# Scores of the undilated group: the 256-column products as three fp32r products, the edges left in fp32

## The chip, the cores and the metric

The kernel runs on one core of one Trainium2 chip. The metric is the device time of one execution in microseconds; three executions of the kernel before took 908.73, 909.21 and 909.42 us, so the median is 909.21 us. The engines are called PE (TensorE: matrix products and transposes), DVE (VectorE), ACT (ScalarE), POOL (GpSimd) and SP (it issues most of the DMAs).

## The reference, cut to what matters

One encoder layer in float32: 512 tokens, width 1024. After a layer norm, one large projection gives queries, keys and values of two kinds of attention; then come an output projection, a cross-attention to 256 memory tokens and a gated feed-forward layer of width 2816. The change lies in the second kind of attention, the dilated mixture, and there in its first group, the one with dilation 1:

```
DIL_SLOTS = 8
DIL_PAIRS = ((128, 1), (512, 4), (2048, 16))
...
for gi, (window, dil) in enumerate(DIL_PAIRS):
    n_side = window // (2 * dil)
    o, lse = banded_attention(to_residue(qb[:, :, gi], dil)[:, :, :, None],
                              to_residue(kb[:, :, gi], dil),
                              to_residue(vb[:, :, gi], dil), n_side)
```

For group 0 (window 128, dilation 1) a query sees the keys within 64 positions on either side: per head a band of scores `q k^T / 8`, a softmax over the band, and a weighted sum of the values. There are 8 heads of 64 columns in the group, which the kernel takes two at a time, as four chunks of 128 columns (c = 0 to 3). The first kind of attention ("window", 8 query heads on 2 key heads, window 128 on each side, with a sink) is also taken in four chunks.

## The kernel before

**Products.** A float32 product is made in one of two ways. Either both operands are float32 and PE is given one matmul, or both are split into a high part of type fp32r (a rounded copy) and a low part (the rest, fp32r too), and PE is given three fp32r products, high·high, high·low and low·high, which add up in PSUM. The projections are of the second kind: `chunk_fm` (L605) makes one 128 x 512 tile of a projection by 8 x 3 = 24 fp32r matmuls of 512 columns. The weights come by DMA into `raw` tiles, ACT copies them to `hi` (L136), DVE subtracts to get `lo` (L138); there are six buffers of each.

**A projected tile.** `proj` (L614) runs `chunk_fm` and then `rope` (L525), which turns the tile from PSUM into SBUF: DVE multiplies by the cosines (L528) and shuffles (L529), POOL multiplies by the sines (L530) and adds (L531). For the queries and keys of the dilated groups the result of L531 is the float32 tile `Q[key]` that the scores use. For the window attention (`"w"` and `"ka"`) the result is split: POOL copies to the high part (L624), DVE subtracts to get the low part (L625).

**Scores of group 0.** `item_a(c)` (L709) makes the scores of one chunk. The two heads j = 0, 1 lie in the two halves of the partitions (`HJ`), so their matmuls use 64 rows of the PE array each, and each has its own PSUM tile `s[j]`. There are four edge matmuls (two per head) of 64 queries by 128 keys, and three blocks u = 1 to 3 of 128 queries by 256 keys, one float32 matmul for each block and head (L719). Then DVE adds the mask and takes the row minimum (L736), ACT takes exponentials (L739), PE transposes the result (`transposes`, L682, L693), ACT copies the transposes to SBUF (`pT`, L698), and PE multiplies by the values (`pv`, L705). `item_w(c)` (L807) does the same for the window attention, with scores by three fp32r products (L820, the pairs in `PAIRS`). It needs the reciprocal of the softmax sums as a tile over the columns: DVE takes the reciprocals `rd` (L843), ACT spreads them over a 128 x 512 tile `rb` of the x pool (L845), and PE transposes that in four pieces (L859), right behind the twenty transposes of the exponentials (sixteen into two `s` tiles, four into the `t` tile). In the text A0 to A3 are the four items of group 0, W0 to W3 those of the window attention, B0 to B3 those of the two other groups.

**Order.** In the attention part PE runs in exactly the order in which the program was written. That order is made by a queue: the projections are written one behind the other, `mmt` counts each matmul as one tick, and an item at the queue's head goes on when its operands have been `ready` long enough in ticks (`LAG` = 24 behind the projection for the float32 tiles, 30 for the split ones). Each `yield` in an item is such a wait. The orders of ACT, DVE and POOL are not written by hand: when the program is built, a scheduler with its own model of durations sorts the instructions of these engines, and the order that it finds is fixed in the program.

**The x pool.** Tiles of 2 KB per partition for all these parts come from one pool with tag `"x"` and 16 buffers (`XB`, L583). `x_tile` (L585) forces queue items if more than 16 are held; `x_free` gives them back.

## Time and profile before

| | us |
|---|---|
| median of three executions | 909.21 |
| lowest, highest | 908.73, 909.42 |
| profiled execution, its time | 908.85 |
| its span (first to last instruction) | 907.10 |
| PE busy | 894.7 |
| DVE busy | 567.3 |
| ACT busy | 384.8 |
| POOL busy | 130.8 |

The attention part that the change touches lies between about 40 and 345 us of the span. "PE" rows are matmuls and transposes; "PEld" rows are the loads of the stationary operand that go ahead of them. A float32 matmul leaves two records of each kind, an fp32r matmul one. A row of the timeline gives the start, the duration, the engine, the source line, the operation with the tile written and the tiles read, the size, how many equal neighbours were merged into the row (x20), and in square brackets how long the engine sat idle before it and who released it. The end of a matmul is modelled, so the pace is read from start to start.

### The profile page before, as it was taken

Reading aid. Unit: us, or ns where it says so; the run is one execution under the profiler, and the core shown is the slowest. Engines: PE = TensorE matmul, PEld = TensorE weight load, DVE = VectorE, ACT = ScalarE, POOL = GpSimd, SP = SyncE. Lnnn points to the kernel's source line nnn. Section 1 sums busy time; section 2 is a strip of 40 time slices with the busy share of each in tenths; the row PEclk is TensorE's granted clock in tenths of the full one; section 3 lists DMA queues with packets and bytes.
Section 4 is the critical chain, followed back from the end, with each engine's and each line's share of the span. In section 5 each row is a group of like instructions: output and inputs, shape, how many; then the busy total and the mean of one; then the engine's idle time right before and its main releaser. Section 6 shows DMA issues by size and latency. Waiting matters only on the chain.

```text
span 907.1 us, 13008 instructions
## 1 busy us (share of the span) xinstructions
PE 894.7 (99%) x5147; PEld 769.8 (85%) x5147; DVE 567.3 (63%) x968; ACT 384.8 (42%) x672; POOL 130.8 (14%) x111
## 2 busy tenths in 40 slices
PE   8999999999999999999999999999999999999996
PEld 7778988898888898788988889899999999888885
DVE  7976146435456667879466576987777767433347
ACT  4563436415545576315454224454444445222200
POOL 1064134332454420010000010000000000000001
PEclk9999999999999999999999999999999999999999
DMA  6762041214221337416222304333333354233201
GB/s 222 228 209 70 25 139 48 73 67 117 70 70 47 94 117 232 140 47 176 80 70 70 94 25 123 88 94 93 101 109 94 98 158 139 94 94 102 82 24 69
DMA packets 117086, 92.84 MB, mean 102 GB/s; under 512 B 12488, under 2 KB 101024, under 8 KB 117026
## 3 DMA queue, kind: packets, MB, share of 16 engines
q1 hardware_dynamic: 116192, 89.80, 32.8%
q10 hardware_dynamic: 834, 2.22, 0.6%
q8 instruction: 40, 0.66, 0.3%
q14 instruction: 20, 0.16, 0.1%
HBM read 87.82 MB, written 4.19 MB: 101 GB/s over the span
## 4 chain that ended last, share of the span: by engine, by line
PE 92%; DVE 4%; DMA 1%; ACT 1%; issue 1%; POOL 0%; DVEq 0%; ACTq 0%
PE g L168 52%; PE s L168 25%; PE o L168 5%; PE t L168 4%; PE o L705 3%; PE s L693 2%; PE s L208 1%; DVE lo L138 1%; DMA vt<-in_ln_in_g_dram 0%; DMA raw<-in_w_up_dram 0%; ACT hi L136 0%; DVE lo L282 0%; DVE oA L348 0%; PE s L1241 0%; DVE st L312 0%
## 5 line engine op out<-in xcount | busy, mean ns | idle before, releaser
L138 DVE TENSOR_TENSOR lo<-raw,hi 128x1024 fp32r<-128x1024 f32 x126 | 159.8, 1270 | 91.1 <-ACT hi L136 90.4
L136 ACT CAST hi<-raw 128x1024 fp32r<-128x1024 f32 x126 | 132.3, 1051 | 145.0 <-PE g L168 86.6
L168 PE MATMUL g<-Thi,hi 128*128 128x512 f32 x240 | 94.8, 395 | 0.0
L168 PE MATMUL g<-Tlo,hi 128*128 128x512 f32 x240 | 94.2, 393 | 0.0
L168 PE MATMUL g<-Thi,lo 128*128 128x512 f32 x240 | 94.0, 392 | 0.0
L109 POOL TENSOR_TENSOR rs<-ve,mhalf 128x1 f32<-128x1 f32 x18 | 15.3, 851 | 521.6 <-DVE ve L115 513.4
L530 POOL TENSOR_TENSOR zs<-zs,rsn 128x512 f32<-128x512 f32 x29 | 56.9, 1963 | 144.6 <-DVE zs L529 131.2
L168 PE MATMUL g<-Uhi,hi 128*128 128x512 f32 (+1 forms) x216 | 74.3, 344 | 0.0
L168 PE MATMUL g<-Ulo,hi 128*128 128x512 f32 (+1 forms) x216 | 74.0, 342 | 0.0
L168 PE MATMUL g<-Uhi,lo 128*128 128x512 f32 (+1 forms) x216 | 73.9, 342 | 0.0
L168 PE MATMUL g<-hi,Thi 128*128 128x512 f32 x184 | 71.6, 399 | 0.0
L168 PE MATMUL g<-hi,Tlo 128*128 128x512 f32 x184 | 71.0, 395 | 0.5 <-DVE Tlo L1189 0.5
L168 PE MATMUL g<-lo,Thi 128*128 128x512 f32 x184 | 70.6, 395 | 0.4 <-DVE lo L282 0.4
L528 DVE TENSOR_TENSOR zs<-g,rc 128x512 f32<-128x512 f32 x29 | 19.9, 687 | 62.1 <-PE g L168 39.6
L168 PE MATMUL g<-x,hi 128*128 128x256 f32 x320 | 58.8, 284 | 0.0
L168 PEld LDWEIGHTS g<-Thi,hi 128*128 128x128 f32 x240 | 45.1, 188 | 10.4 <-issue 0.8
L168 PEld LDWEIGHTS g<-Tlo,hi 128*128 128x128 f32 x240 | 45.1, 188 | 9.7 <-issue 0.8
L168 PEld LDWEIGHTS g<-Thi,lo 128*128 128x128 f32 x240 | 45.1, 188 | 9.3
L168 PEld LDWEIGHTS g<-x,hi 128*128 128x128 f32 x320 | 50.0, 192 | 0.5 <-issue 0.3
L168 PE MATMUL s<-Ulo,hi 128*128 128x512 f32 (+1 forms) x136 | 49.5, 364 | 0.0
L168 PE MATMUL s<-Uhi,hi 128*128 128x512 f32 (+1 forms) x136 | 49.5, 364 | 0.0
L168 PE MATMUL s<-Uhi,lo 128*128 128x512 f32 (+1 forms) x136 | 49.5, 364 | 0.0
(378 smaller groups left out, 2075.7 us busy)
## 6 DMA issues: line engine op xcount, KB each, us to landing
raw<-in_w_in_dram SPq DMA_DIRECT2D x37, 512.0 KB, 3.8
raw<-in_w_gate_dram SPq DMA_DIRECT2D x22, 512.0 KB, 3.8
raw<-in_w_up_dram SPq DMA_DIRECT2D x22, 512.0 KB, 4.0
raw<-in_w_down_dram SPq DMA_DIRECT2D x22, 512.0 KB, 3.5
raw<-in_w_xk_dram SPq DMA_DIRECT2D x8, 512.0 KB, 3.8
raw<-in_w_xv_dram SPq DMA_DIRECT2D x8, 512.0 KB, 3.4
raw<-in_w_xq_dram SPq DMA_DIRECT2D x8, 512.0 KB, 4.6
raw<-in_w_xo_dram SPq DMA_DIRECT2D x8, 512.0 KB, 3.5
```

Of the source, the lines that this page charges most:

```text
L109: nc.gpsimd.tensor_tensor(out_, in_, mhalf, ALU.pow)
L136: nc.scalar.copy(hi, raw)
L138: (eng or nc.vector).tensor_tensor(lo, raw, hi.bitcast(F32), ALU.subtract)
L168: on_pe(nc.tensor.matmul(o, l, r, start=first, stop=last))
L208: on_pe(nc.tensor.transpose(ps[:, i // 4, f : f + P], t[:, i * P : (i + 1) * P], ident))
L528: nc.vector.tensor_tensor(zc, ps, rc, ALU.mult)
L530: nc.gpsimd.tensor_tensor(sh, sh, rsn, ALU.mult)
L693: nc.tensor.transpose(tp[:, k, :], s_, ident)
L705: nc.tensor.matmul(o[HJ[j], t0:t1], lhs(j), rhs(j), start=i == 0, stop=i == len(parts) - 1)
```

## The change

The keys and queries of group 0 (`key[1] == 0`) are now split in `proj` like those of the window attention: POOL makes the high part (8 casts of 128 x 512 more), DVE the low part (8 subtractions of 128 x 512 more), and they count as ready 30 ticks after the projection instead of 24. The float32 tile is kept as the third part. In `item_a` each of the six 256-column float32 matmuls of a chunk becomes three fp32r products; the loop over the two heads moves inside, so that a block is done for both heads before the next. The four edge matmuls of a chunk still use the float32 tiles. A chunk's key and query so hold three tiles of the x pool each instead of one, and the pool grows from 16 to 18 buffers, wherever it is used.

```diff
-            raw = [xpool.tile([P, 1, 512], F32, tag="x", bufs=16, name="raw") for _ in range(2)]
+            raw = [xpool.tile([P, 1, 512], F32, tag="x", bufs=18, name="raw") for _ in range(2)]
...
-    XB = 16
+    XB = 18
...
         ps = chunk_fm(key, wt)
-        if key[0] not in ("w", "ka"):
+        group = key[0] not in ("w", "ka")
+        if group and key[1]:
             Q[key] = x_tile([P, S], F32, key)
             rope(ps, view, Q[key])
             ready[key] = now[0] + LAG
             return
-        raw = x_tile([P, S], F32, "raw")
+        raw = x_tile([P, S], F32, key if group else "raw")
         rope(ps, view, raw)
         hi, lo = Q[key] = dest or [x_tile([P, S], F32R, key) for _ in range(2)]
         nc.gpsimd.tensor_copy(hi, raw)
         nc.vector.tensor_tensor(lo, raw, hi.bitcast(F32), ALU.subtract)
-        x_free("raw")
+        if group:
+            Q[key] = (hi, lo, raw)
+        else:
+            x_free("raw")
         ready[key] = now[0] + LAG + 6
...
-                mm(s[j][o0 : o0 + 64, 0, 0:P], q[HJ[j], q0 : q0 + 64], k[HJ[j], kk0 : kk0 + P], True, True)
+                mm(s[j][o0 : o0 + 64, 0, 0:P], q[2][HJ[j], q0 : q0 + 64], k[2][HJ[j], kk0 : kk0 + P], True, True)
         for u in range(1, 4):
             bk, c0 = cols[u]
-            for j in range(2):
-                mm(
-                    s[j][:, bk, c0 : c0 + 256],
-                    q[HJ[j], 128 * u - 64 : 128 * u + 64],
-                    k[HJ[j], 128 * (u - 1) : 128 * (u + 1)],
-                    True,
-                    True,
-                )
+            for i, (m, n) in enumerate(PAIRS):
+                for j in range(2):
+                    mm(
+                        s[j][:, bk, c0 : c0 + 256],
+                        q[m][HJ[j], 128 * u - 64 : 128 * u + 64],
+                        k[n][HJ[j], 128 * (u - 1) : 128 * (u + 1)],
+                        i == 0,
+                        i == 2,
+                    )
```

The same 16 becomes 18 in two later uses of the pool, in the feed-forward layer. In PE's order the scores of A0, A2 and A3 now stand six projection matmuls later than before, A1 where it stood. The twenty-four transposes of each W item stand in PE's order as before, those of W1 six matmuls later; the four of the tile `rb` are still the last of them. The orders of the other engines changed with the build. Line numbers of the changed kernel are up to 5 higher than those of the kernel before (L693 is now L697, L698 is L702, L845 is L850, L862 is L867, L624 and L625 are L625 and L626).

On ACT, around the transposes of W0, these rows stood before. `x<-rd` is the copy that makes `rb`, `pT` are the copies of the transposed exponentials, `fw` is the copy of the transposed `rb`:

```order
L136 CAST hi<-raw 128x1024
L845 COPY x<-rd 128x512
L698 COPY pT<-s 128x512 x4
L698 COPY pT<-t 128x512
L862 COPY fw<-o 128x512
L669 COPY vg<-g 128x512
```

Now the same place reads:

```order
L136 CAST hi<-raw 128x1024
L702 COPY pT<-s 128x512 x4
L702 COPY pT<-t 128x512
L850 COPY x<-rd 128x512
L867 COPY fw<-o 128x512
L673 COPY vg<-g 128x512
```

The copy that makes `rb` moved from ahead of the five `pT` copies to behind them.

On ACT, around the transposes of W1, this stood before (the first row is the last three exponentials of W1):

```order
L833 ACTIVATE pu,dnW<-pu,ast 128x385 x3
L136 CAST hi<-raw 128x1024
L845 COPY x<-rd 128x512
L698 COPY pT<-s 128x512 x4
L698 COPY pT<-t 128x512
L862 COPY fw<-o 128x512
```

And this stands there now:

```order
L838 ACTIVATE pu,dnW<-pu,ast 128x385
L136 CAST hi<-raw 128x1024
L838 ACTIVATE pu,dnW<-pu,ast 128x385 x2
L136 CAST hi<-raw 128x1024
L702 COPY pT<-s 128x512 x2
L850 COPY x<-rd 128x512
L702 COPY pT<-s 128x512 x2
L702 COPY pT<-t 128x512
L867 COPY fw<-o 128x512
```

Here the copy that makes `rb` moved behind the first two `pT` copies, and two casts of weights moved up, one of them in between the exponentials. In W2 and W3 it stands ahead of the `pT` copies, as before.

On POOL, at the start of the attention part, the rope and the split of the first tiles stood like this before (`x_466` is the key of chunk 0, `x_496` its query, `kah_435` the high part of the window attention's key):

```order
L530 TENSOR_TENSOR zs_98<-zs_98,rsn_71 128x512
L531 TENSOR_TENSOR x_466<-zs_98 128x512
L530 TENSOR_TENSOR zs_98<-zs_98,rsn_71 128x512
L531 TENSOR_TENSOR x_496<-zs_98 128x512
L530 TENSOR_TENSOR zs_98<-zs_98,rsn_71 128x512
L531 TENSOR_TENSOR x_564<-zs_98 128x512
L624 CAST kah_435<-x_564 128x512
```

And like this now (`x_500` is the query, `x_471` and `x_505` are the two high parts):

```order
L530 TENSOR_TENSOR zs_98<-zs_98,rsn_71 128x512
L531 TENSOR_TENSOR x_466<-zs_98 128x512
L625 CAST x_471<-x_466 128x512
L530 TENSOR_TENSOR zs_98<-zs_98,rsn_71 128x512
L531 TENSOR_TENSOR x_500<-zs_98 128x512
L625 CAST x_505<-x_500 128x512
L530 TENSOR_TENSOR zs_98<-zs_98,rsn_71 128x512
L531 TENSOR_TENSOR x_540<-zs_98 128x512
L625 CAST kah_435<-x_540 128x512
```

Each tile's cast stands right behind the addition that makes it, so the rope of the query comes one cast later. On DVE the two low parts of chunk 0 (L626) stand behind the weights' subtraction that follows the query's shuffle, and behind the shuffle of the next tile; the second of them is ahead of the next weights' subtraction (L138).

## The prediction

> **What bounds the kernel now.** I read the page first, then the waits of PE in the attention part, then the timelines of PE, ACT, POOL and DVE around the items that the change touches. On the page PE is busy nearly all the time, and the chain that ended last is PE work:

> ```profile
> PE 894.7 (99%) x5147; PEld 769.8 (85%) x5147; DVE 567.3 (63%) x968; ACT 384.8 (42%) x672; POOL 130.8 (14%) x111
> PE 92%; DVE 4%; DMA 1%; ACT 1%; issue 1%; POOL 0%; DVEq 0%; ACTq 0%
> ```

> All waits of PE between 40 and 345 us are three:

> ```profile
> PE s L168 <- POOL x L531: 0.5, 1, 0.5
> PE s L693 <- ACT pu L785: 0.3, 1, 0.3
> PE s L168 <- DVE x L625: 0.2, 1, 0.2
> ```

> So in this part a microsecond of PE work that goes is a microsecond won, and a microsecond for which PE waits is one lost; the other engines count only where PE waits for them. Half a microsecond of waiting is already in A0, where the scores wait for the query.

> **The scores.** In A0 the timelines of PE and of PEld show one chunk (eight records of the four edge matmuls, twelve of the six large ones):

> ```profile
> 55.62 0.39 PE L168 MATMUL g<-Tlo,hi 128*128 128x512 f32 x1
> 55.85 0.39 PE L168 MATMUL g<-Thi,lo 128*128 128x512 f32 x1
> 56.70 1.95 PE L168 MATMUL s<-x 64*64 64x128 f32 x20 [0.46 <-POOL x L531]
> 58.57 0.50 PE L168 MATMUL g<-Thi,hi 128*128 128x512 f32 x1
> ```

> ```profile
> 56.69 0.21 PEld L168 LDWEIGHTS s<-x 64*64 64x64 f32 x8 [0.88 <-POOL x L531]
> 57.07 1.17 PEld L168 LDWEIGHTS s<-x 64*128 64x128 f32 x12 [0.17 <-issue]
> ```

> The large ones last from 57.07 to the next projection matmul at 58.57, which is 1.50 us. What three fp32r products cost at this shape stands in W1, whose first two blocks have 64 rows and 256 columns too, two heads at a time (a row x4 holds two products):

> ```profile
> 149.23 0.39 PE L168 MATMUL s<-kah,x 64*128 64x256 f32 x2
> 149.45 0.28 PE L168 MATMUL s<-kal,x 64*128 64x256 f32 x2
> 149.57 0.40 PE L168 MATMUL s<-kah,x 64*128 64x256 f32 x4
> 149.81 0.28 PE L168 MATMUL s<-kal,x 64*128 64x256 f32 x2
> ...
> 150.75 0.33 PE L168 MATMUL t<-kal,x 64*128 64x384 f32 x1
> 150.92 0.34 PE L168 MATMUL t<-kah,x 64*128 64x384 f32 x1
> 151.19 0.50 PE L168 MATMUL g<-Tlo,hi 128*128 128x512 f32 x1
> ```

> The first pair takes 0.22 us (149.45 - 149.23), each further one 0.12 (149.57 - 149.45, and 0.24 for two up to 149.81). The last one before a projection costs 0.10 more than its pace (151.19 - 150.92 = 0.27 against 150.92 - 150.75 = 0.17). Nine pairs: 0.22 + 8 x 0.12 + 0.10 = 1.28 us. Saved: 1.50 - 1.28 = 0.22 us a chunk, **0.88 us** in four. Bounds: 0.32 a chunk if the edges ahead hide the 0.10 by which the first pair is slower, 0.02 if that is paid at each of the three blocks. I take 0.22, since a W item pays it once.

> **A0's wait.** How soon scores can follow a projection is seen in A2, where they waited for nothing:

> ```profile
> 136.53 0.39 PE L168 MATMUL g<-Thi,lo 128*128 128x512 f32 x1
> 136.85 1.95 PE L168 MATMUL s<-x 64*64 64x128 f32 x20
> ```

> That is 0.32 us, so in A0 they could have begun at 55.85 + 0.32 = 56.17 and lost 56.70 - 56.17 = 0.53. The new order puts six projection matmuls ahead, 6 x 0.23 = 1.38 (pace from 55.62 to 55.85), so they can begin at 57.55. POOL and DVE at this place:

> ```profile
> 49.18 1.30 POOL L530 TENSOR_TENSOR zs<-zs,rsn 128x512 f32<-128x512 f32 x1 [21.14 <-DVE zs L529]
> 50.56 2.35 POOL L531 TENSOR_TENSOR x<-zs 128x512 f32<-128x512 f32 x1
> 53.11 2.17 POOL L530 TENSOR_TENSOR zs<-zs,rsn 128x512 f32<-128x512 f32 x1 [0.20 <-DVE zs L529]
> 55.36 1.28 POOL L531 TENSOR_TENSOR x<-zs 128x512 f32<-128x512 f32 x1
> ...
> 61.39 0.61 POOL L624 CAST kah<-x 128x512 fp32r<-128x512 f32 x1
> ```

> ```profile
> 52.92 1.21 DVE L138 TENSOR_TENSOR lo<-raw,hi 128x1024 fp32r<-128x1024 f32 x1
> ...
> 56.95 0.72 DVE L529 STREAM_SHUFFLE zs<-g 128x512 f32<-128x512 f32 x1
> ...
> 63.71 0.67 DVE L625 TENSOR_TENSOR kal<-x,kah 128x512 fp32r<-128x512 f32 x1
> ```

> The key's tile ends at 52.91, its cast (0.61), 0.08 behind as POOL's operations follow each other in these rows, at 53.60, so the query's rope begins at 53.68 instead of 53.11 and its tile ends at 57.21 instead of 56.64. That is ahead of 57.55: the edges don't wait. They take 57.07 - 56.69 = 0.38, to 57.93. The query's cast ends at 57.21 + 0.08 + 0.61 = 57.90, DVE is done with the shuffle at 57.67, and its subtraction ends about 57.95 + 0.67 = 58.62. The block's third product needs it, and would begin at 57.93 + 0.22 + 0.12 = 58.27; with the 0.05 that PE took after POOL's end (56.69 - 56.64) it begins at 58.67. Lost: 0.40 instead of 0.53, a gain of **0.13**. Bounds: no wait at all, a gain of 0.53; or one more DVE subtraction of 1.21 in the way, a loss of 1.08.

> The POOL rows show how uncertain that is: the same operation took 1.30 us alone and 2.17 beside the DVE subtraction. [...]

> In the other chunks the split is early enough. The other 6 casts and 6 subtractions (0.61 and 0.67 us each) lie in gaps of POOL and DVE, a projection or more ahead of their use. The pool of 18 buffers costs nothing that I can see: PE never waits for one now.

> **The moved copies.** This is the largest term. ACT and DVE around W0:

> ```profile
> 89.06 0.61 ACT L845 COPY x<-rd 128x512 f32<-128x512 f32 x1
> 91.86 2.05 ACT L698 COPY pT<-s 128x512 f32<-128x512 f32 x4 [2.19 <-PE s L693]
> 93.78 0.63 ACT L698 COPY pT<-t 128x512 f32<-128x512 f32 x1
> 94.25 0.64 ACT L862 COPY fw<-o 128x512 f32<-128x512 f32 x1
> ```

> ```profile
> 88.25 0.20 DVE L843 RECIPROCAL rd<-dnW 128x8 f32<-128x8 f32 x1 [1.25 <-ACT pu L833]
> ```

> and PE's transposes of `rb`, load and product:

> ```profile
> 92.87 0.47 PEld L859 LDWEIGHTS o<-cst,x 128*128 128x128 f32 x4
> ```

> ```profile
> 92.97 0.60 PE L859 MATMUL o<-cst,x 128*128 128x128 f32 x4
> ```

> Before, `rb` was made at 89.06, three microseconds ahead of need. Now its copy stands behind five `pT` copies, and the first of these waits for PE's transposes. It then takes the slot that `fw` had: it starts at 94.25 and ends at 94.86, and PE's load can begin at 94.91 instead of 92.87. PE executes in order, so the projection behind it waits too: **2.04 us** lost. The values' products of W0 come 14 projection matmuls later and stay covered.

> In W1 two `pT` copies stand ahead of it:

> ```profile
> 160.11 2.06 ACT L698 COPY pT<-s 128x512 f32<-128x512 f32 x4 [2.58 <-PE s L693]
> 162.02 0.63 ACT L698 COPY pT<-t 128x512 f32<-128x512 f32 x1
> ```

> ```profile
> 161.22 0.60 PE L859 MATMUL o<-cst,x 128*128 128x128 f32 x4
> ```

> A copy there takes (162.02 - 160.11) / 4 = 0.48. `rb` would start at 160.11 + 0.96 = 161.07, end at 161.68 and let the load begin at 161.73; it needs 161.22 less the 0.10 between load and product in W0. Lost: **0.61 us**. Bounds of the two together: 2.4 (PE could use an overlap of 0.1 each) to 3.0 (the weight cast put ahead of W1's copies delays them).

> **The sum.** -0.88 - 0.13 + 2.04 + 0.61 = +1.64 us. Against the profiled execution's 908.85 that is 910.5; its time lies 0.36 below the median of the three, so against the median it is 909.21 + 1.64 = 910.9 us, 0.18% more. A measurement of this kernel can tell about 0.2%, here 1.8 us, from no change. Moved to its bounds alone, the scores' term gives 910.5 to 911.7, A0's 910.5 at the low end, the copies' 910.6 to 911.2; all low ends together give 909.8.

> **The rivals.** *The copy is not in the way.* `rd` is there at 88.45, and ACT then idles 2.19 us. If ACT took the ready copy ahead of the waiting ones, no stall would come: -0.88 - 0.13 gives 908.2 us. Against it: before, too, ACT stood idle in front of its first `pT` copy, and no row shows it passing over a waiting instruction; it could not, though, be seen there, as nothing behind was ready. [...] Chance 0.07.

> *POOL and DVE get in each other's way in A0.* If one more 1.21 us subtraction lies ahead of the query's low part, A0 costs 1.08 instead of gaining 0.13: 909.21 + 1.64 + 1.21 = 912.1 us, slower beyond doubt. It decides from 0.2 us on, since 1.64 is so near 1.8. For it: the spread from 1.30 to 2.17. Against it: the new order puts the low part ahead of the next weights' subtraction. Chance 0.16.

> *The products are not cheaper.* If nine pairs behind float32 edges cost as much as six float32 ones, 0.88 is gone: 911.7 us. W1 speaks against it. Chance 0.03.

> **The numbers.** The forecast has 0.74. In it the time passes 1.8 us more in somewhat over a third of the cases (0.27), by the bounds; with the second rival and most of the third, slower has 0.45. Faster needs the first rival and a far better A0: 0.02. The rest, 0.53, is within 0.2%. The range leaves out the first rival and goes 0.2 us, the least distance of an execution from the median of the three, beyond the low ends together (909.8) and the second rival (912.1): 909.6 to 912.3.

> **What would show it.** In the changed profile: PE idle about 2 us ahead of the transposes of `rb` in W0 and 0.6 in W1, released by the ACT copy; A0's scores waiting for the low part, some 0.4 us; the large products of a chunk 1.28 us from first load to the next projection. No wait of PE for ACT in W0 would make the forecast wrong, and so would one of more than half a microsecond anywhere else.

## The result, and the profile after

The changed kernel takes **915.48 us** (median of six, 912.76 to 916.17) against 908.8 us for the kernel before (908.4 to 909.42): a ratio of 1.0066 on record, with a 95% interval from 1.0056 to 1.0075 (that of the two medians is 1.0074). It is slower by 6.7 us where 1.7 were forecast, and beyond the range. The profiled execution took 915.7 us with a span of 913.6; that of before took 908.85 with a span of 907.1. So 6.85 us have to be found, 6.5 in the span and 0.35 outside it.

The page of the changed kernel shows PE busy for 4.3 us more than before, though its work was to shrink, and idle for 2.2 us more (the span's 6.5 less those 4.3):

```profile
PE 899.0 (98%) x5171; PEld 773.2 (85%) x5171; DVE 576.7 (63%) x976; ACT 384.7 (42%) x672; POOL 136.1 (15%) x119
PE 90%; DVE 4%; ACT 2%; DMA 1%; issue 1%; POOL 1%; DVEq 0%; ACTq 0%; POOLq 0%
```

The waits of PE (total, times, longest) give the idle part. Two rows are new at the top, and they are the two places of the forecast. They make 3.8 us; the 0.5 us of A0's wait before and a wait of 1.1 us for a DMA at the start of the program are gone, which leaves 2.2:

```profile
PE o L864 <- ACT x L850: 2.3, 2, 1.8
PE s L168 <- DVE x L626: 1.5, 2, 1.3
```

The first is the transposes of `rb` in W0 and W1, the second the scores' wait for a low part, nearly all of it in A0.

The busy part is the surprise. Cut into the stretches of 3.41 us at whose edges the granted clock changes, the windows of the changed kernel show it in the column PEclk, the third from the end (PE's busy time is the first value after the stretch's length):

```profile
58.18:61.60 3.42, 1.98 (x27) 1.43 (x20) 3.06 (x2) 0.64 (x1) 3.28 (x4) 1.00 0.96 386
61.60:65.01 3.41, 3.41 (x9) 2.63 (x9) 3.41 (x18) 2.25 (x10) 1.38 (x1) 0.50 0.41 122
65.01:68.42 3.41, 3.41 (x22) 2.96 (x22) 3.38 (x8) 2.86 (x10) 0.81 (x2) 1.00 0.20 61
95.73:99.14 3.41, 1.58 (x11) 1.34 (x10) 0.69 (x1) 2.61 (x6) 1.15 (x2) 1.00 0.36 107
99.14:102.56 3.42, 3.42 (x10) 2.73 (x9) 0.00 (x0) 0.73 (x2) 0.00 (x0) 0.50 0.00 0
102.56:105.97 3.41, 3.41 (x30) 2.13 (x31) 0.00 (x0) 0.00 (x0) 0.00 (x0) 1.00 0.00 0
```

In 58.18 to 61.60 PE is idle for 1.44 us, in 95.73 to 99.14 for 1.83 us, and behind each of them stands one stretch at half the clock, in which 9 or 10 matmuls are done. By offsets (the start of the same 128x512 product in the two traces) 1.71 us are lost in the first and 1.52 in the second, and the page counts them as busy. In the kernel before, the clock reads full from 3.97 us to 905 us.

Not every execution has both. Two of the six took 912.76 us at a mean granted clock of 0.997, the other four 915.25 to 916.17 us at 0.993 to 0.995. Two such windows alone take 2 x 3.41 x 0.5 / 913.6 = 0.0037 off that mean, so in the two shorter ones at least one window was missing; only the 915.7 was profiled.

A0 on PE, with the wait for the low part and the projection's slow matmuls behind it:

```profile
58.56 0.50 PE L168 MATMUL s<-x 64*128 64x256 f32 x4 [0.17 <-POOL x L625]
60.34 1.09 PE L168 MATMUL s<-x 64*128 64x256 f32 x14 [1.27 <-DVE x L626]
61.36 0.62 PE L168 MATMUL g<-Thi,hi 128*128 128x512 f32 x1
61.78 0.63 PE L168 MATMUL g<-Tlo,hi 128*128 128x512 f32 x1
```

Those come every 0.42 us here and came every 0.23 before. What the scores waited for is on DVE, and beside it, on POOL, the next rope's first step:

```profile
58.54 1.74 DVE L626 TENSOR_TENSOR x<-x 128x512 fp32r<-128x512 f32 x1 [0.49 <-POOL x L625]
60.20 2.31 DVE L138 TENSOR_TENSOR lo<-raw,hi 128x1024 fp32r<-128x1024 f32 x1
```

```profile
57.90 0.61 POOL L625 CAST x<-x 128x512 fp32r<-128x512 f32 x1
58.47 1.27 POOL L530 TENSOR_TENSOR zs<-zs,rsn 128x512 f32<-128x512 f32 x1
```

POOL goes from the query's cast straight to the rope of `ka` at 58.47. DVE's subtraction starts at 58.54 and takes 1.74 us, where the same operation took 0.67 in the profile of before.

W0 on ACT and on PE. The copy of `rb` (L850) stands behind five `pT` copies:

```profile
94.85 2.06 ACT L702 COPY pT<-s 128x512 f32<-128x512 f32 x4 [2.69 <-PE s L697]
96.76 0.63 ACT L702 COPY pT<-t 128x512 f32<-128x512 f32 x1
97.24 0.66 ACT L850 COPY x<-rd 128x512 f32<-128x512 f32 x1
```

```profile
97.95 0.66 PE L864 MATMUL o<-cst,x 128*128 128x128 f32 x4 [1.83 <-ACT x L850]
98.37 0.60 PE L168 MATMUL g<-lo,Thi 128*128 128x512 f32 x1
...
169.34 0.66 PE L864 MATMUL o<-cst,x 128*128 128x128 f32 x4 [0.44 <-ACT x L850]
```

The projection behind W0's transposes waited with them, until 98.37. The last row is W1, with 0.44 us. The scores themselves came out as forecast; in A2, from the first large load to the next projection's product:

```profile
144.98 1.13 PEld L168 LDWEIGHTS s<-x 64*128 64x128 f32 x18 [0.17 <-issue]
```

```profile
146.25 0.50 PE L168 MATMUL g<-Thi,hi 128*128 128x512 f32 x1
```

146.25 - 144.98 = 1.27 us, where the forecast had 1.28.

### The profile page after: what moved, and what is told of

Same layout as the page of the kernel before. It is cut to its first block, busy times and chain, and to the rows that moved or that the text cites. A ratio compares the mean times of both kernels' runs of the same rounds, so it can differ in the third digit from the quotient of the medians.

```text
span 913.6 us, 13069 instructions
## 1 busy us (share of the span) xinstructions
PE 899.0 (98%) x5171; PEld 773.2 (85%) x5171; DVE 576.7 (63%) x976; ACT 384.7 (42%) x672; POOL 136.1 (15%) x119
## 4 chain that ended last, share of the span: by engine, by line
PE 90%; DVE 4%; ACT 2%; DMA 1%; issue 1%; POOL 1%; DVEq 0%; ACTq 0%; POOLq 0%
PE g L168 50%; PE s L168 24%; PE o L168 5%; PE t L168 4%; PE o L709 3%; PE s L697 2%; DVE lo L138 1%; ACT hi L136 1%; PE s L208 1%; DMA vt<-in_ln_in_g_dram 0%; DMA raw<-in_w_up_dram 0%; POOL x L531 0%; DMA raw<-in_w_in_dram 0%; ACT pT L702 0%; DVE lo L282 0%
## 5 line engine op out<-in xcount | busy, mean ns | idle before, releaser
L138 DVE TENSOR_TENSOR lo<-raw,hi 128x1024 fp32r<-128x1024 f32 x126 | 161.7, 1286 | 94.3 <-ACT hi L136 93.6
L168 PE MATMUL g<-Thi,hi 128*128 128x512 f32 x240 | 95.4, 398 | 0.0
L168 PE MATMUL g<-Tlo,hi 128*128 128x512 f32 x240 | 95.0, 396 | 0.0
L168 PE MATMUL g<-Thi,lo 128*128 128x512 f32 x240 | 94.5, 394 | 0.0
L530 POOL TENSOR_TENSOR zs<-zs,rsn 128x512 f32<-128x512 f32 x29 | 53.8, 1856 | 141.9 <-DVE zs L529 135.9
L168 PE MATMUL g<-Uhi,hi 128*128 128x512 f32 (+1 forms) x216 | 74.3, 344 | 0.0
L168 PE MATMUL g<-Ulo,hi 128*128 128x512 f32 (+1 forms) x216 | 74.0, 342 | 0.0
L168 PE MATMUL g<-Uhi,lo 128*128 128x512 f32 (+1 forms) x216 | 73.9, 342 | 0.0
L168 PE MATMUL g<-hi,Thi 128*128 128x512 f32 x184 | 72.2, 402 | 0.0
L168 PE MATMUL g<-hi,Tlo 128*128 128x512 f32 x184 | 71.6, 399 | 0.5 <-DVE Tlo L1194 0.5
L168 PE MATMUL g<-lo,Thi 128*128 128x512 f32 x184 | 71.4, 399 | 0.4 <-DVE lo L282 0.4
L168 PE MATMUL g<-x,hi 128*128 128x256 f32 x320 | 58.8, 284 | 0.0
L168 PEld LDWEIGHTS g<-Thi,hi 128*128 128x128 f32 x240 | 45.5, 190 | 10.2 <-issue 0.5
L168 PEld LDWEIGHTS g<-Thi,lo 128*128 128x128 f32 x240 | 45.5, 190 | 9.5
L168 PEld LDWEIGHTS g<-Tlo,hi 128*128 128x128 f32 x240 | 45.4, 189 | 9.5 <-issue 0.5
L168 PEld LDWEIGHTS g<-x,hi 128*128 128x128 f32 x320 | 50.0, 192 | 0.5 <-issue 0.3
L168 PE MATMUL s<-Uhi,hi 128*128 128x512 f32 (+1 forms) x136 | 49.5, 364 | 0.0
L168 PE MATMUL s<-Ulo,hi 128*128 128x512 f32 (+1 forms) x136 | 49.5, 364 | 0.0
L168 PE MATMUL s<-Uhi,lo 128*128 128x512 f32 (+1 forms) x136 | 49.5, 364 | 0.0
```

The lines of the kernel that those rows point to most:

```text
L138: (eng or nc.vector).tensor_tensor(lo, raw, hi.bitcast(F32), ALU.subtract)
L168: on_pe(nc.tensor.matmul(o, l, r, start=first, stop=last))
L530: nc.gpsimd.tensor_tensor(sh, sh, rsn, ALU.mult)
```

## The experiments

Two theories stood against each other. **Theory H**: a long wait of TensorE costs its length, and then a window of 3.41 us at half the clock. **Theory L**: a wait costs its length and nothing else, and what is missing is in the new work. A second question was why A0's low part came late. Where the text counts offsets, it is by the start of the same 128x512 product in two traces.

### The copy of rb put back ahead

```diff
-        nc.scalar.copy(
+        rbc = nc.scalar.copy(
             rb.rearrange("p b (j d) -> p (b j) d", j=2),
...
-        t0, *t1, t3, t2 = transposes(
+        with tc.issue_after(rbc.ins):
+            t0, *t1, t3, t2 = transposes(
```

> The changed kernel with one thing put back: in the sink group's items the copy of the reciprocals (rb) stands ahead of the five pT copies on ScalarE again, as it did before the change. Theory H (a long wait of TensorE costs its own length and then a 3.41 us window at half the granted clock, 1.7 us more): W0's wait of 1.83 us and W1's of 0.44 us go, the half-clock window behind W0 goes, the one behind A0 stays; 915.5 - 1.83 - 0.44 - 1.7 = 911.5 us. Theory L (a wait costs its length and nothing else, and the missing 3.4 us are in the new work itself, so they stay): 915.5 - 2.3 = 913.2 us.

Measured: **909.79 us** (909.24 to 912.08), 1.0016 of before (1.0007 to 1.0025). ACT of this kernel has the copy ahead of the transposes' copies again, and PE's list of waits has no row for L850:

```profile
90.07 0.62 ACT L850 COPY x<-rd 128x512 f32<-128x512 f32 x1
92.85 2.06 ACT L702 COPY pT<-s 128x512 f32<-128x512 f32 x4 [2.16 <-PE s L697]
```

The gain is 5.7 us, more than the 4.0 of theory H and far more than the 2.3 of theory L, which falls: the waits that went are 2.3 us long. The rest is not one half-clock window but two. A0's wait is as long as it was, but in the profiled execution the grid of windows falls so that 1.27 us of idle time lie in one of them, and the next keeps the full clock:

```profile
57.35:60.77 3.42, 2.15 (x28) 1.36 (x27) 3.10 (x3) 1.24 (x1) 3.28 (x4) 1.00 0.96 340
60.77:64.18 3.41, 3.41 (x20) 2.74 (x17) 3.41 (x16) 1.84 (x9) 1.73 (x2) 1.00 0.41 137
```

Six of the eleven times lie between 909.24 and 909.79, the other five between 910.66 and 912.08, about a half-clock window higher, as if A0's wait costs its window in some executions and not in others. The mean granted clock fits it, 0.997 to 0.999 in the six and 0.995 to 0.997 in the five, but only one of them was profiled, so that reading is argued.

### A0's scores 14 products later

```diff
-        ready[key] = now[0] + LAG + 6
+        ready[key] = now[0] + LAG + 6 + (14 if group and key[2] == 0 else 0)
```

> The changed kernel with A0's scores asked for 14 chunk matmuls (some 3.2 us) later, so that the query's low part is there in time; all else as it is. Theory H: A0's wait of 1.44 us goes, and the half-clock window behind it with its 1.7 us; the one behind W0 stays: 915.5 - 1.44 - 1.7 = 912.4 us. Theory L: 915.5 - 1.4 = 914.1 us.

Measured: **913.5 us** (913.1 to 914.05), 1.0051 (1.0039 to 1.0063), between the two. The wait for the low part is gone, but the edit put another in its place, so its time decides nothing. A0's softmax (L741 on DVE) came so late that the normalisation of the memory rows went ahead of it, and PE's transposes waited for it:

```profile
PE s L697 <- DVE stT L741: 2.4, 1, 2.4
```

```profile
62.65 1.29 DVE L131 BATCH_NORM_STATS2 st<-oB 128x6 f32<-128x512 f32 x2 [0.51 <-DMA oB<-in_mem_dram]
...
66.87 0.28 DVE L741 CUSTOM_DVE_ANT_0 pu<-s,cst 128x128 f32<-128x128 f32 x1
```

What it does show is the grid. The new wait is cut in two by it (1.46 and 1.08 us idle), W0's 1.83 us too (its larger part leaves 1.50), and no window at half clock follows either:

```profile
64.86:68.27 3.41, 1.95 (x9) 1.29 (x7) 3.41 (x13) 2.46 (x7) 0.57 (x1) 1.00 0.09 28
68.27:71.69 3.42, 2.34 (x15) 1.74 (x16) 2.97 (x10) 3.42 (x14) 1.52 (x3) 1.00 0.00 0
71.69:75.10 3.41, 3.41 (x23) 2.60 (x23) 1.13 (x3) 2.08 (x4) 0.19 (x1) 1.00 0.55 159
95.58:98.99 3.41, 1.91 (x10) 1.91 (x11) 0.46 (x1) 2.04 (x4) 0.00 (x0) 1.00 0.00 0
98.99:102.41 3.42, 3.42 (x22) 2.71 (x22) 0.00 (x0) 0.59 (x1) 0.00 (x0) 1.00 0.00 0
```

### Both edits

> The changed kernel with both edits: rb's copy ahead of the pT copies, and A0's scores 14 chunk matmuls later. Theory H: no window at half clock inside the program, and only the cheaper scores are left: 908.8 - 0.88 - 0.46 (A0's wait of the kernel before goes too) = 907.5 us, up to 908.4 if A0 keeps half a microsecond of wait. Theory L: 915.5 - 2.3 - 1.4 = 911.8 us.

Measured: **912.08 us** (911.37 to 912.25), 1.0033 (1.0021 to 1.0045). That is near theory L's number, but not for its reason: the softmax's wait is here too, this time in one window, and the next runs at half clock.

```profile
67.26:70.67 3.41, 0.97 (x8) 0.86 (x9) 3.41 (x19) 3.01 (x13) 0.43 (x1) 1.00 0.00 0
70.67:74.09 3.42, 3.42 (x12) 2.59 (x13) 1.03 (x1) 2.62 (x8) 1.33 (x3) 0.50 0.33 95
```

The edit that was meant to free A0 was a bad one; the experiment with `va` below frees it in another way.

### The kernel before, with W0's copy made late

```diff
+        if c == 0:
+            with tc.issue_after(pcopy[0].ins):
+                spread()
         two = ps_tile("o", 1, [P, 4, P])
```

(`spread` holds the copy of `rb`, `pcopy[0]` the last `pT` copy; the other items call it where it stood.)

> The kernel before the change with one thing spoiled: in W0 alone the copy of the reciprocals stands behind the five pT copies on ScalarE. None of the change's products, splits or buffers is in it. Theory H: TensorE waits some 1.8 us in W0 and the next 3.41 us window runs at half the granted clock: 908.8 + 1.8 + 1.7 = 912.3 us. Theory L: 908.8 + 1.8 = 910.6 us and no such window. Rival: the half clock needs the change's longer scores as well as a wait; then also 910.6 us.

Measured: **911.02 us** (910.28 to 912.73), 1.0026 (1.0017 to 1.0035). The profiled execution, the 912.73, shows the wait and the window:

```profile
PE o L869 <- ACT x L849: 1.8, 1, 1.8
```

```profile
93.25:96.67 3.42, 1.59 (x12) 1.35 (x11) 0.00 (x0) 2.62 (x6) 0.63 (x1) 1.00 0.36 104
96.67:100.08 3.41, 3.41 (x10) 2.66 (x10) 0.00 (x0) 0.83 (x2) 0.00 (x0) 0.50 0.00 0
```

Just ahead of W0 it stands 0.60 us behind the kernel before, after the window 4.18: of these 3.58 us, 2.06 come at the wait and 1.52 in the window. So neither the change's products nor its splits are needed for the half clock; the rival falls. The median of the times, 2.4 us over before, is less than that, and the lowest is 1.6 us over. In four of the other executions (910.86 to 911.43 us) the mean granted clock is 0.999, and one such window alone would bring it to 1 - 3.41 x 0.5 / 911 = 0.998: there the wait cost no window. For the rest that stays open, as they weren't profiled.

### No rope beside the query's low part

`va` is projected ahead of `ka`, with the copy of `rb` put back ahead as above.

```diff
-        proj(("ka",), w_cols(w_in, KA), NAT, kaT)
         proj_va()
+        proj(("ka",), w_cols(w_in, KA), NAT, kaT)
```

> The changed kernel with the rb copy ahead of the pT copies, and with va projected ahead of ka, so that no rope addition of GpSimd stands beside the subtraction that makes the query's low part (va needs none). Theory P (the subtraction took 1.74 us because GpSimd's next rope step ran beside it): the subtraction takes 0.69 us again, A0's second wait falls from 1.27 to 0.2 or 0.3 us, and no window runs at half clock in any run; 909.5 - 1.0 = 908.5 us. Rival: the subtraction is slow for another reason, such as its place behind DVE's own work; the wait stays and the time too, 909.8 us.

Measured: **908.47 us** (907.19 to 909.54), 1.0001 (0.9992 to 1.001). The subtraction of the query's low part and PE's wait for it:

```profile
58.39 0.69 DVE L626 TENSOR_TENSOR x<-x 128x512 fp32r<-128x512 f32 x1 [1.86 <-POOL x L625]
```

```profile
59.14 1.10 PE L168 MATMUL s<-x 64*128 64x256 f32 x14 [0.22 <-DVE x L626]
```

0.69 us and 0.22 us, as theory P had them; the rival falls. In the profiled execution no window at half clock is left inside the program (mean granted clock 0.997, half only behind the end of PE's work). The key's low part, which still has a rope step beside it, still takes 1.77 us, but PE doesn't wait for that one. This is the changed kernel with both of its side effects mended, and it isn't measurably faster than the kernel before.

### Chunk 0 left in fp32

Chunks 1 to 3 have the three products, chunk 0 the code of before; the copy of `rb` stands ahead.

```diff
-        if group and key[1]:
+        if group and (key[1] or key[2] == 0):
```

> The changed kernel with the rb copy ahead of the pT copies, and chunk 0 left as it was before (fp32 scores, no split), so that only chunks 1 to 3 have the three products. A0's wait should be that of the kernel before, 0.5 us. By the sum: three times 0.22 us saved, and some 0.35 us more that the changed kernels spend outside the span: 908.66 - 0.66 + 0.35 = 908.35 us. Rival: the saving is an illusion of where I cut the rows, and the time is 909.0 us.

Measured: **908.46 us** (907.99 to 909.17), 0.9997 (0.9988 to 1.0005). That is 0.1 us from the sum and 0.5 from the rival. The interval reaches to 909.1 us, so the time alone doesn't exclude the rival; the offsets do, by which its A1, A2 and A3 save 0.18, 0.25 and 0.23 us.

### The buffers alone

```diff
-    XB = 16
+    XB = 18
```

(and the four other uses of 16)

> The kernel before the change with 18 of the x buffers in place of 16, and nothing else. Theory: the buffers cost nothing in the span and nothing outside it, 908.66 us, and what the changed kernels spend more outside the span (2.13 against 1.78 us) comes with their instructions. Rival: the buffers bring the 0.35 us, 909.0 us; or they let transfers start sooner and change the span by a few tenths either way.

Measured: **908.78 us** (907.59 to 909.51), 1.0003 (0.9994 to 1.0012), with 1.76 to 1.85 us outside the span. The buffers cost nothing that can be measured.

### Waits put into a dense stretch

```diff
             gemm_fm(pg, wg, h2T, 0, S)
+            if f in HOLD:
+                for i in range(HOLD[f]):
+                    nc.scalar.copy(dz[:, 0:512], pg)
+                nc.tensor.transpose(ps_tile("t", 1)[:, 0:P], dz[:, 0:P], ident)
             gemm_fm(pu, wu, h2T, 0, S)
```

with `HOLD = {6: 1, 8: 2, 10: 3, 12: 2, 14: 3, 16: 4, 18: 2, 20: 3, 21: 6}`.

> The kernel before the change with nine waits put into TensorE's stream in the gate and up products, where its matmuls otherwise stand end to end: after a gate product one to six ScalarE copies in a row of the finished tile, and a TensorE transpose that needs the last of them, so that TensorE stands still for some 0.9 us (one copy) to 4 us (six). The output stays what it was. Theory H: where the idle time inside one 3.41 us window of the clock's grid is over some 1.5 us the next window runs at half the granted clock, where it is less none does, and a wait of 2 us may go free when the grid cuts it in two. Rival: the half clock belongs to the attention items with their short fp32 matmuls; here no window but those with over 3 us of idle time is followed by one.

Measured: 930.44 us in the profiled execution, 928.63 in the other. Three of the nine waits, window by window:

```profile
638.44:641.85 3.41, 1.40 (x7) 0.90 (x6) 1.92 (x2) 2.97 (x5) 0.00 (x0) 1.00 0.28 84
641.85:645.26 3.41, 3.41 (x9) 2.64 (x9) 1.50 (x2) 0.93 (x2) 0.00 (x0) 0.50 0.53 154
710.12:713.53 3.41, 1.67 (x8) 1.05 (x6) 1.89 (x3) 2.53 (x4) 0.00 (x0) 1.00 0.48 139
713.53:716.95 3.42, 2.53 (x12) 2.12 (x13) 1.87 (x3) 1.73 (x4) 0.00 (x0) 1.00 0.51 151
734.01:737.42 3.41, 1.75 (x8) 1.13 (x6) 1.89 (x3) 2.45 (x4) 0.00 (x0) 1.00 0.49 145
737.42:740.84 3.42, 1.84 (x9) 1.53 (x10) 1.20 (x2) 2.15 (x4) 0.00 (x0) 1.00 0.48 143
```

The window with 2.01 us of idle time (3.41 - 1.40) halves the next, and the rival, for which it took 3 us or the attention items, falls. Windows with 1.74 and 1.66 us don't, nor does a wait of 3.2 us that the grid cuts into 1.66 and 1.58. So theory H is right in kind, but its 1.5 us isn't a fixed limit: 1.44 us sufficed behind A0 in the changed kernel, 1.74 didn't here. What else than idle time decides it stays open.

The ends of the programs narrow it down, where PE's work stops within a window of the grid. The kernel before kept the full clock behind a window with 1.81 us of idle time; the one with W0's copy made late lost it behind 1.89:

```profile
898.26:901.67 3.41, 1.60 (x14) 1.40 (x12) 2.04 (x6) 0.00 (x0) 0.26 (x1) 1.00 0.00 0
901.67:905.09 3.42, 0.00 (x0) 0.00 (x0) 2.50 (x6) 0.00 (x0) 0.66 (x1) 1.00 0.25 90
902.21:905.63 3.42, 1.53 (x13) 1.33 (x12) 2.05 (x6) 0.00 (x0) 0.34 (x1) 1.00 0.00 0
905.63:909.04 3.41, 0.00 (x0) 0.00 (x0) 2.42 (x6) 0.00 (x0) 0.58 (x1) 0.50 0.27 97
```

Other ends agree: 1.75 us (the changed kernel) and 1.77 (the doubled products below) kept it, 2.39 (18 buffers) and 2.40 (`va` ahead) lost it; the mean granted clock of these two executions, 0.997 each for 0.999 in the kernel before, fits that. In the whole traces of before and after, and in the windows given here of the others, every window with 1.83 us or more idle was followed by one at half clock, and none with 1.81 or less was, but for the 1.44 behind A0. The work in that one is A0's score products of 64 rows. Whether these count for less was not tested; the same products with 1.27 us idle, in the kernel with the copy put back, kept the clock.

### What lies outside the span

In every profiled or timed execution of the kernel before, 1.74 to 1.86 us lie between its time and its span; in the changed kernel and its variants with all four chunks split, 2.0 to 2.2. Four kernels looked for it. The first two are the kernel before with eight one-column fills on POOL, and with each of the 24 large score products issued twice (the second writes the same values).

```diff
+            if not key[1]:
+                nc.gpsimd.memset(small, 0.0)
```

> The kernel before the change with eight more GpSimd instructions and nothing else: a one-column fill behind the rope of each key and query of the undilated group, eight in all, as many as the change adds in casts. The question is the time outside the span, 1.78 us in every run of the kernel before and 2.13 us in those of the changed kernel. If it comes with GpSimd's instructions it is 2.1 us here; if not, 1.78 us. The span should stay at 906.8 us, within the few tenths by which single runs differ.

```diff
-            for j in range(2):
+            for j in (0, 1, 0, 1):
```

> The kernel before the change with each of the 24 score products of 256 columns issued twice (the second writes the same values), so that TensorE has 24 instructions more, as many as the change gives it, and no other engine has any. If the time outside the span comes with TensorE's instructions it is 2.1 us here; if not, 1.78 us. The span grows by twelve fp32 products' time on each half of the array, some 4 times 1.3 us as the fp32 scores of 256 columns took it in the profile of before, so to about 912 us.

Measured: **914.94 us** (1.007, 1.0047 to 1.0093) and **918.85 us** (1.0111, 1.0082 to 1.014), with 1.74 to 1.9 us outside the span. So neither POOL's nor PE's instructions bring it here. The doubled products cost 1.29 to 1.31 us in each of A1, A2 and A3, as expected; in A0 the late softmax brought waits and a window at half clock again, behind 1.94 us of idle time.

The surprise is 6 us for eight tiny fills, which the scheduler put at the program's start. They add no wait. The products got slower: between 800 and 880 us one of 512 columns took 0.389 us in the kernel before and 0.395 with the fills.

```profile
L168 PE MATMUL s<-hi 128*128 128x512 f32 x70 | 27.2, 389 | 0.0
```

```profile
L168 PE MATMUL s<-hi 128*128 128x512 f32 x64 | 25.3, 395 | 0.0
```

The tile that they fill is one column wide, 4 bytes a partition, and can shift what is allocated behind it. So the third kernel made that tile 16 columns wide, and the fourth had the fills on VectorE, into the wide tile.

```diff
-    small = spool.tile([P, 1], F32, tag="small", bufs=1, name="small")
+    small = spool.tile([P, 16], F32, tag="small", bufs=1, name="small")
```

> The kernel before the change with the eight one-column GpSimd fills, now into the first column of a tile 16 columns wide (64 bytes a partition) in place of one of one column (4 bytes); the fills, as the earlier run's, are issued at the program's start. If the 6 us of the earlier run, in which every product of 512 columns from the cross attention's end on took 0.396 us for 0.389, came from the 4 bytes that shift the tiles allocated behind them, the time is back at 908.7 us; if from the instructions themselves, it stays at 915 us.

> The kernel before the change with eight one-column VectorE fills into a tile 16 columns wide, at the program's start: as many more instructions as the change gives VectorE. If the time outside the span comes with VectorE's instructions, it is 2.1 us; if not, 1.78 us, and then what brings the 0.35 us to the changed kernels stays open. The span should be that of the kernel before, 906.8 us.

Measured: **910.2 us** (909.6 to 912.73; 1.0017, 1.0003 to 1.0031) and **910.8 us** (909.93 to 911.37; 1.0026, 1.0014 to 1.0037). Neither 908.7 nor 915: the same fills with 15 columns more cost 4.7 us less, with the engines' instructions in the same order, so the place of the tiles matters. But what the 15 columns win back is not the pace of the 512-column products. With 64 bytes these are as slow, by GpSimd's fills and by VectorE's:

```profile
L168 PE MATMUL s<-hi 128*128 128x512 f32 x67 | 26.6, 397 | 0.0
```

It is products of 256 columns that got faster: between 620 and 750 us one of `g<-x,hi` takes 0.276 us with 64 bytes, 0.281 with 4 and 0.283 in the kernel before. By offsets the third kernel gains 1.3 us from 611 to 758 us, where the second loses 1.2; from 758 to 890 both lose 3.9, with no wait to show for any of it. Whether the slower 512-column products come with the tile or with the fills stays open, as no kernel has the tile without fills. Outside the span the third kernel has 1.77 to 1.83 us, the one with VectorE's fills 1.90 to 2.07. So some 0.2 of the 0.35 us come with as many VectorE instructions as the change adds, if its subtractions count like fills; the rest is open.

## Why the prediction was wrong

**The sum, term by term**, in the profiled executions:

| term | forecast, us | measured, us | where measured |
|---|---|---|---|
| scores, four chunks | -0.88 | -0.83 | offsets over A1, A2, A3: -0.17, -0.25, -0.20; a mean one for A0 |
| A0's wait | -0.13 | +0.91 | 0.17 + 1.27, less the 0.53 |
| W0 | +2.04 | +2.05 | offset over its transposes; 1.83 in the list of waits |
| W1 | +0.61 | +0.64 | offset over W1; 0.44 of it in the list of waits |
| windows at half clock | 0 | +3.23 | offsets: 1.71 behind A0, 1.52 behind W0 |
| outside the span | 0 | +0.35 | 915.7 - 913.6, against 908.85 - 907.1 |
| start of the program | 0 | +0.41 | offset ahead of A0; -0.2 to 0.75 in the other kernels |
| sum | +1.64 | +6.76 | of 6.85 |

**The step that failed first** is in the premise: "a microsecond for which PE waits is one lost". In this kernel it can be two. The waits of A0 and W0 each left one window of the clock's grid half idle, and the window behind each ran at half the clock, which cost 1.71 us more behind A0 and 1.52 more behind W0. The forecast put that term at nothing. The profile of before couldn't show it, since its longest wait in this part is 0.46 us; the forecast took the price of a long wait over from short ones. The late copy in the kernel before shows the price without any of the change, in its profiled execution (3.58 us for a wait of 1.83), and the copy put back shows it from the other side (5.7 us won for 2.3 us of waits).

A window need not be idle as a whole for that: 1.44 us of idle time in it sufficed behind A0, 1.83 behind W0 and 2.44 in the kernel with both edits.

**The second step that failed** is the size of A0's term: "its subtraction ends about 57.95 + 0.67". It started at 58.54, 0.59 later (0.41 of it the later start of everything ahead), and took 1.74 us, with POOL's rope step of 1.27 us beside it. PE's wait of 1.27 us for it is also what the forecast itself named as a sign of being wrong, one of more than half a microsecond at another place. The order on POOL was known, since the next rope stands right behind the query's cast; the forecast counted on DVE's duration from a row that had nothing beside it. The subtraction lasts about 0.5 us beyond the end of POOL's step at 59.74, and takes 0.69 us without that step beside it, in the kernel with `va` ahead. The second rival (chance 0.16) had the effect in kind, a microsecond more in A0, though by another subtraction in the way. With that alone the forecast would have been 911.9 us, and the measured time less the 3.23 us of the two windows is 912.25: both inside the range. The clock put it outside.

**What held.** The scores save 0.21 us a chunk where 0.22 was forecast, so the third rival, that they aren't cheaper, falls. W0's and W1's waits came at the place, by the cause and nearly at the size forecast. The first rival, that the copy isn't in the way, falls with the wait's row; ACT did not take the ready copy first: `rd` was there at 91.46, ACT then idled for 2.69 us, and the copy started at 97.24, behind the five others. The 18 buffers cost nothing (908.78 us against 908.61).

**What the change is worth** without its side effects: 908.47 against 908.61 us, no difference that can be measured. The median span of that kernel is 906.3 us against 906.8, so the products do save time there, but 0.36 us of it is lost again outside the span.

## What to carry to other kernels

Before a wait is priced at its length, lay the windows of the granted clock over the trace: a stall that left 1.83 us or more of one window idle (in one case 1.44) halved the clock for the next 3.41 us here, and whether a stall did so depended on where the grid fell (W0's wait of 1.83 us did with all of it in one window, and not with 1.50), so the times of one kernel spread. When a change adds splits on GpSimd and VectorE, take the duration of each from a row where the other engine works beside it (here 1.74 us for 0.67), and look what GpSimd does next. When a scheduler places the work, compare the order on every engine, not only where the edit is: here the one copy that moved cost more than the edited products saved.
